# A hybrid encoder layer on one core: deferred use of transferred blocks, lanes tied behind the main stream, and earlier loads of token sums

## The chip, the cores and the metric

The kernel runs on one core of one Trainium2 chip. The core has a matrix engine (TensorE, PE), whose weight load runs beside its matmuls (PEld), a vector engine (VectorE, DVE), an activation engine (ScalarE, ACT), GpSimd (POOL) and SyncE (SP), and 16 DMA engines that move data between DRAM and the core's own memory. Each engine carries out its instructions in order; an instruction may wait for others on semaphores, and what is behind it waits too. SP issues nearly all transfers here, in one queue; POOL issues those that add into their target. The metric is the device time of one execution in microseconds (us).

## The reference

One encoder layer is computed for two sequences, a sample of 1024 tokens and a prompt of 512, with `d_model` 2048 and everything in float32:

```
h = rms_norm(x, norm_g);  z = h @ w_in                       # 2048 -> 5632
c_val, c_glu, c_gate, q, k, v, a_gate = split(z)             # 1024 x3, 1024, 256, 256, 1024
conv = silu(layer_norm(depthwise_conv31(c_val * sigmoid(c_glu)) + b)) @ w_pw * silu(c_gate)
attn = banded_sink_attention(rope(q), rope(k), v, sink) * silu(a_gate)   # 8 heads, 2 kv heads, window 128
y = rms_norm(x + concat(conv, attn) @ w_out, final_norm_g)
```

## The kernel before, in words

**Products.** Every float32 operand is split into a high and a low part, and a product is three passes on PE: high × high, high × low, low × high. The split of a weight block of 512 KB is a `Prep`: SP loads `raw`, ACT copies the high part (L343), DVE subtracts to get the low part (L344), and the result is an `hl` tile. There are three `raw` and three `hl` tiles.

**Units.** The input projection of the sample is cut into 22 column-block pairs: 8 of the convolution (`conv`) and 14 others (`rest`: gates, k and v, q with the attention gate). Each is worked on in two `Unit`s, one per half of the 2048 inputs. A `Unit` is a 2×2 scheme with seven products instead of eight: column blocks (two) by token halves (two, of 512 tokens). Weight sums (`sub`, DVE L132) and token sums (`T`, tiles t) are its operands. One product is four blocks of 128 by three passes, twelve matmuls (L178), into one of three banks in the order a b a c a c a; bank a is added into throughout, so the third product in a (step 4) may start only when the second (step 2) has been read, and so on. Reading a bank is the `tap`: after steps 0, 2, 3 and 6 an ACT copy (L203) into a new tile, after steps 1, 4 and 5 a DVE add (L205) to such a tile. The tiles are taken in turn from two pools, g and u, of four buffers each (`E`).

The tap of a product is traced in the midst of the next one. After steps 1, 4, 5 and 6 one of the unit's four output blocks is ready. In the first of the two `Unit`s of a pair it is stored to DRAM (`part_...`). In the second, POOL issues a transfer that adds the stored part into the tile (`add_into`, L334), and `done`, traced at once behind it, works on the sum: for conv `gated` (DVE L686, ACT L687, DVE L688 and the product L692), for q, k and v `rope` (DVE L753 to L756) or a scale, for gates and the attention gate a scale (DVE L701) and a silu (ACT L706). Then SP stores the block.

**Order of the stages.** 8 conv units on the first half of the inputs (to 188 us of the profile); 8 conv units on the second half, with `done` (188 to 378); 14 rest units on the second half (378 to 653); 14 rest units on the first half, with `done` (653 to 1049); then the prompt as `Job`s (L444, with its own taps, gates, q, k, v), and the `Post`s, which do the attention output and the last projection. The first two units of three of these stages run as a pair, product by product in turn. The 28 tiles of token sums hold one half of the inputs; at the end of the first and of the third stage `switch` replaces them, step by step: behind the unit's product of a step, `follow` makes that step's sum of the new half from four loaded tiles (`token_sum`, ACT L346 or L343, DVE L347 or L344) and then loads the four tiles of the next step (`load_sum`, L616) into the four p buffers. At the last unit before the prompt, another `follow` splits the prompt's x the same way from tiles `f` loaded one pair ahead (L1304).

**Lanes.** Depthwise convolution (`taps`: 29 DVE instructions L725 per block of 128 channels, 1024 wide), attention, and preparations such as the normalisation are generators on three `Lane`s. `tick`, called for each piece of a product, gives a lane credit, and the lane is traced a step further when it has enough. The scheduler orders each engine's instructions by priority, and by trace order within that: weight preparation, taps, `done` and token sums are `urgently` traced, with a higher priority than the lanes. A lane's instruction whose operands are ready early can be placed ahead of the stream's.

Of the kernel before, what the change touches and what calls it, by code (L numbers as in the profile page):

```python
# [2 lines left out]

# [32 lines left out]
SOON = 800  # L36
PM = 30
RUSH = 1.2
SPREAD = 3
RATES = (0.4, 0.9, 0.3, 1.0)  # L40
S1, S2, S3, S4, S5, S6, S7 = 5000, 6000, 9000, 7000, 3500, 2500, 6000
# [13 lines left out]
class Lane:  # L55


    def __init__(self, rate=1.0):
        self.todo = deque()
        self.rate = rate  # L60
        self.credit = 0.0
# [3 lines left out]

    def step(self):
        try:
            self.credit -= next(self.todo[0]) or 0
        except StopIteration:
            self.todo.popleft()  # L70

# [10 lines left out]
class Unit:  # L82
# [82 lines left out]
    def product(self, step, late):  # L165
        e, nc = self.e, self.e.nc
        p, o = OPERAND[step]
        i = self.at[p]
        e.w_prep(i + 1)
        hl = e.hl[i]  # L170
        n = BANK[step]
        if step in FRESH:
            self.bank[n] = e.PS(self.tags[n], [W])
        acc = self.bank[n]
        toks = e.T[SUMS[step]]
        for j in range(HALF):
            for q, (l, r) in enumerate(((0, 0), (0, 1), (1, 0))):
                nc.tensor.matmul(  # L178
                    acc,
                    hl[:, l, o, j, :],  # L180
                    toks[j][:, r],
                    start=step in FRESH and j == 0 and q == 0,
                    stop=step in LAST and j == HALF - 1 and q == 2,
                    skip_group_check=True,
                )
            if j == 0:
                for fn in late:
                    fn()
                e.w_prep(i + NHL)
            e.tick(3 * MM)  # L190
        if step in (1, 3, 5, 6):
            e.hl.pop(i)
        for fn in self.after.get(step, ()):
            fn()
        return [lambda: e.urgently(self.tap, step)]

    def tap(self, step):
# [8 lines left out]
        if step in (1, 4, 5, 6):  # L206
            part, d = self.part[n[0]][n[1]], self.d.pop(n)
            if self.done:

                e.add_into(d, part)  # L210
                self.done(n[0], n[1], d)
            else:
                e.store(part, d)

# [51 lines left out]
class Encoder:  # L266
    def __init__(self, ctx, tc, a):
# [8 lines left out]
        self.conv = Lane()  # L276
        self.attn = Lane()
        self.prep = Lane()
        self.lanes = [self.attn, self.conv, self.prep]
        self.turn = False  # L280
        self.banks = 0
# [67 lines left out]
    def tick(self, ns):  # L349
        for lane in self.lanes:  # L350
            lane.tick(ns)


    def constants(self):
# [63 lines left out]
    def run(self, items):  # L418
# [3 lines left out]
        for n, item in enumerate(items):  # L422
# [3 lines left out]
            if isinstance(item[0], Unit):  # L426
                for u in item:
                    u.open()
                for step in range(7):
                    for u in item:  # L430
                        late = u.product(step, late)
                continue
            job = item[0]
            job.acc = [self.acc()]
            nk = len(job.ks)
            for q in range(0, nk, 2 * HALF):
# [3 lines left out]
                for kk in range(2 * HALF):  # L440
# [9 lines left out]
                        )  # L450
                    if kk == 0:
                        self.w_prep(at + NHL)
                    if i in job.ticks:
                        job.ticks[i]()
                    self.tick(3 * MM)
# [58 lines left out]
class Sequence:  # L514
# [88 lines left out]
                e.store(self.sums_d[g, name][j], t)  # L603
            yield 6000

    def load_sum(self, name, g):
        e = self.e
        out = []
        for j in range(HALF):
            x = e.PT("p", NP, [W])  # L610
            if name in ("S1", "S2", "S3", "S4"):
                src = self.sums_d[g, name][j]
            else:
# [598 lines left out]
def encoder(ctx, tc, a):  # L1212
# [44 lines left out]
    def switch(unit, g):  # L1257
# [13 lines left out]
        for step in range(7):  # L1271
            unit.after[step] = [lambda step=step: follow(step)]

# [140 lines left out]
```

## Time and profile before

| | |
|---|---|
| three runs | 2347.69, 2348.84, 2353.24 us; median 2348.84 |
| the profiled execution | 2354.78 us; its span 2353.0 us |
| mean granted clock of PE | 0.965 |
| PE, DVE, ACT, POOL busy | 2186.8, 1613.1, 971.7, 76.9 us |
| DMA | 434.73 MB, mean 185 GB/s |
| the stretches 188 to 378, 378 to 653, 653 to 728.5, 728.5 to 1049, 1049 to the end | 190.4, 274.9, 75.2, 320.2, 1304.3 us |

The profile shows one execution. Busy time is time in which an engine works on an instruction; a share of it is of the whole span or of a window. Rows that read "X <- Y" give time that X stood idle until Y released it. Tiles are named by their pool, with their number left out. An instruction on a 1024-wide tile and one on a 512-wide tile of the same line stand in one group unless the shape is shown.

### The profile page before, as it was taken

To read this page: it belongs to the slowest core of one execution; us is meant where nothing else is said; L and a number is where in the kernel's file an instruction comes from. 1 tells how busy PE (TensorE), PEld (TensorE's weight loads), DVE (VectorE), ACT (ScalarE), POOL (GpSimd) and SP (SyncE) were. 2 spreads that over 40 slices of the span, in tenths; PEclk is the share of its full clock that TensorE was granted. 3 is DMA by queue.
4 is the path that set the end of the run, shared out by engine and by line. 5 is a ranking of instruction groups with operands and counts; after the bars stand their busy time and mean duration, and the time that the engine had idled before them with its cause. 6 is when DMAs were issued, how large, how long until landed. Compare 5 with 4: busy or idle time off the path is not lost.

```text
span 2353.0 us, 26578 instructions
## 1 busy us (share of the span) xinstructions
PE 2186.8 (93%) x9510; PEld 1781.2 (76%) x9510; DVE 1613.1 (69%) x2475; ACT 971.7 (41%) x1488; POOL 76.9 (3%) x92
## 2 busy tenths in 40 slices
PE   7999888999967878879999999999999999999998
PEld 5877667888845756667888888888787778888886
DVE  8657777999997777766636677867675367636343
ACT  5465324333443222244335454754464354423232
POOL 0001110000001111110000000000000000000000
PEclk8999899999989988889999999999999999999999
DMA  8988757664566556577655565455724438526442
GB/s 290 329 277 227 195 129 230 210 234 166 165 197 170 143 156 156 152 224 246 205 175 157 190 216 172 155 169 188 257 82 157 134 123 289 166 95 226 132 134 72
DMA packets 220421, 434.73 MB, mean 185 GB/s; under 512 B 20352, under 2 KB 78080, under 8 KB 220288
## 3 DMA queue, kind: packets, MB, share of 16 engines
q1 hardware_dynamic: 207616, 409.96, 52.5%
q0 software_dynamic: 12672, 23.07, 6.3%
q8 instruction: 74, 1.21, 0.2%
q14 instruction: 59, 0.48, 0.1%
HBM read 311.32 MB, written 121.63 MB: 184 GB/s over the span
## 4 chain that ended last, share of the span: by engine, by line
PE 57%; issue 22%; DMA 9%; DVE 7%; POOL 3%; ACT 2%; SPq 1%; POOLq 0%; ACTq 0%; DVEq 0%
PE a L444 17%; PE c L444 9%; PE b L444 9%; PE a L178 5%; DMA u<-q_d 3%; PE c L178 2%; PE s L835 2%; DVE f L725 2%; PE a L1174 2%; PE s L1174 2%; DVE hl L344 2%; POOL g L334 2%; PE pv L867 2%; DMA raw<-w_in 1%; DMA u<-ag_d 1%
## 5 line engine op out<-in xcount | busy, mean ns | idle before, releaser
L178 PE MATMUL a<-t,hl 128*128 128x512 f32 x1968 | 514.9, 415 | 105.0 <-DVE u L205 40.5
L178 PEld LDWEIGHTS a<-t,hl 128*128 128x128 f32 x1968 | 394.7, 203 | 204.3 <-DVE u L205 44.5
L444 PE MATMUL a<-t,hl 128*128 128x512 f32 x2112 | 506.4, 392 | 0.0
L444 PEld LDWEIGHTS a<-t,hl 128*128 128x128 f32 x2112 | 394.0, 188 | 79.9
L725 DVE SCALAR_TENSOR_TENSOR f<-f,c_w_dw,f 128x1024 f32<-128x1024 f32 (+1 forms) x464 | 452.4, 1013 | 2.7 <-ACT f L720 2.2
L343 ACT ACTIVATE hl<-raw 128x1024 fp32r<-128x1024 f32 (+1 forms) x279 | 275.9, 990 | 431.1 <-PE a L444 82.8
L344 DVE TENSOR_TENSOR hl<-raw,hl 128x1024 fp32r<-128x1024 f32 (+1 forms) x279 | 317.7, 1139 | 159.7 <-ACT hl L343 154.6
L178 PE MATMUL c<-t,hl 128*128 128x512 f32 x984 | 248.7, 400 | 20.1 <-DVE t L344 7.7
L444 PE MATMUL b<-t,hl 128*128 128x512 f32 x1056 | 258.5, 395 | 3.7 <-ACT t L346 1.9
L444 PE MATMUL c<-t,hl 128*128 128x512 f32 x1056 | 252.9, 391 | 0.0
L178 PEld LDWEIGHTS c<-t,hl 128*128 128x128 f32 x984 | 188.9, 193 | 65.2 <-DVE t L344 11.3
L444 PEld LDWEIGHTS b<-t,hl 128*128 128x128 f32 x1056 | 198.0, 190 | 45.2 <-ACT t L346 2.7
L444 PEld LDWEIGHTS c<-t,hl 128*128 128x128 f32 x1056 | 197.1, 188 | 39.9
L253 ACT ACTIVATE hl<-raw 128x1024 fp32r<-128x1024 f32 x88 | 93.0, 1058 | 118.3 <-PE a L444 45.3
L178 PE MATMUL b<-t,hl 128*128 128x512 f32 x492 | 119.2, 390 | 0.2
L178 PEld LDWEIGHTS b<-t,hl 128*128 128x128 f32 x492 | 92.2, 188 | 20.4 <-DVE t L347 0.8
L132 DVE TENSOR_TENSOR raw<-raw,raw 128x512 f32<-128x512 f32 x123 | 84.4, 686 | 23.9 <-DMA raw<-w_in 20.8
L344 DVE TENSOR_TENSOR a<-pt,a 128x512 fp32r<-128x512 f32 x64 | 44.1, 689 | 73.5 <-ACT a L343 73.3
L343 ACT ACTIVATE a<-pt 128x512 fp32r<-128x512 f32 x64 | 38.1, 595 | 90.3 <-PE pt L872 89.9
L1174 PE MATMUL a<-hl,t 128*128 128x512 f32 x192 | 74.7, 390 | 0.0
L203 ACT ACTIVATE u<-a 128x512 f32<-128x512 f32 x56 | 33.4, 596 | 97.7 <-PE a L178 95.9
L835 PE MATMUL s<-t,a 128*128 128x384 f32 (+1 forms) x288 | 59.4, 335 | 14.4 <-ACT a L343 13.8
(237 smaller groups left out, 2198.5 us busy)
## 6 DMA issues: line engine op xcount, KB each, us to landing
raw<-w_in SPq DMA_DIRECT2D x169, 512.0 KB, 5.0
raw<-w_out SPq DMA_DIRECT2D x64, 512.0 KB, 3.7
raw<-w_out SPq DMA_DIRECT2D x64, 256.0 KB, 3.3
raw<-w_pw SPq DMA_DIRECT2D x24, 512.0 KB, 3.5
f<-xT_s SPq DMA_DIRECT2D x38, 256.0 KB, 5.8
low_conv<-hl SPq DMA_DIRECT2D x16, 512.0 KB, 3.2
f<-x_s SPq DMA_DIRECT2D x16, 512.0 KB, 6.3
p<-sum_S SPq DMA_DIRECT2D x32, 256.0 KB, 3.8
```

Source lines behind the costliest of these rows:

```text
L132: self.e.nc.vector.tensor_tensor(out, x, y, ALU.subtract)
L178: nc.tensor.matmul(acc, hl[:, l, o, j, :], toks[j][:, r], start=step in FRESH and j == 0 and q == 0, stop=step in LAST and j == HALF - 1 a ...
L203: nc.scalar.activation(self.d[n], bank, AF.Copy)
L253: e.nc.scalar.activation(t[:, 0], raw, AF.Copy)
L334: self.nc.gpsimd.dma_start(dst, src, accum_op=ALU.add)
L343: nc.scalar.activation(hi, x, AF.Copy)
L344: nc.vector.tensor_tensor(lo, x, hi.bitcast(F32), ALU.subtract)
L444: nc.tensor.matmul(job.acc[0], hl[:, l, kk // HALF, kk % HALF, :], r, start=i == 0 and p == 0, stop=i == nk - 1 and p == 2,)
L725: nc.vector.scalar_tensor_tensor(t, h[:, j : j + T], w(j), t, ALU.mult, ALU.add)
L835: nc.tensor.matmul(ps[:, 0:n], qs[:, x, h], k[y][:, keys], start=p == 0, stop=p == 2)
L867: nc.tensor.matmul(pv, v[x][:, vs], pt[:, y], start=i == 0 and p == 0, stop=i == last and p == 2)
L1174: nc.tensor.matmul(acc, self.mix[self.KS[i]][:, m, b * P : (b + 1) * P], part[l].rearrange("p a b -> p (a b)"), start=i == 0 and p == 0, s ...
```

## The change

It has four parts. Line numbers in the changed kernel are 3 or 4 higher up to the tap (L178 becomes L181, L203 and L205 become L207 and L209), 6 higher for the weight preparation (L343, L344 become L349, L350), and 43 higher from the rope and the taps on (L725 becomes L768).

1. `done` is not traced behind `add_into`. It is put into `e.later` with a count, `LANDING = 4`; `turn_over`, called once in each product right behind the tap and the weight preparation, lowers the counts and traces what has come to zero. What is left is traced at the first `Job`.
2. `mark` notes the last DVE and the last ACT instruction traced so far (at each `turn_over`); `behind` ties everything traced within it to come after these two in the engines' order. Lane steps and deferred `done`s are traced in it.
3. In `switch`, loads run two steps ahead instead of one, and for odd steps go into tiles of pool `a`, two pairs of two, instead of the four of `p`.
4. The prompt's x goes to tiles of pool `a`, and is loaded three pairs ahead instead of one.

```diff
+LANDING = 4
 class Lane:
-    def __init__(self, rate=1.0):
+    def __init__(self, e, rate=1.0):
+        self.e = e
...
     def step(self):
         try:
-            self.credit -= next(self.todo[0]) or 0
+            with self.e.behind():
+                self.credit -= next(self.todo[0]) or 0
...
                 for fn in late:
                     fn()
                 e.w_prep(i + NHL)
+                e.turn_over()
             e.tick(3 * MM)
...
                 e.add_into(d, part)
-                self.done(n[0], n[1], d)
+                e.later.append([LANDING, lambda: self.done(n[0], n[1], d)])
...
+    def mark(self):
+        found = {}
+        for i in reversed(self.nc.cur_bb.bb.instructions):
+            if i.engine in (mybir.EngineType.DVE, mybir.EngineType.Activation):
+                found.setdefault(i.engine, i)
+                if len(found) == 2:
+                    break
+        self.marks = list(found.values())
+    @contextmanager
+    def behind(self):
+        with ExitStack() as stack:
+            for i in self.marks:
+                stack.enter_context(self.tc.issue_after(i))
+            yield
+    def turn_over(self, all=False):
+        self.mark()
+        for n, entry in enumerate(self.later):
+            entry[0] -= 1
+        while self.later and (all or self.later[0][0] <= 0):
+            with self.behind():
+                self.urgently(self.later.popleft()[1])
...
+            while self.later:
+                self.turn_over(True)
             job = item[0]
...
                     if kk == 0:
                         self.w_prep(at + NHL)
+                        self.turn_over()
...
-    def load_sum(self, name, g):
+    def load_sum(self, name, g, wide):
+        if wide:
+            pairs = [e.A([2, W], F32) for _ in range(HALF // 2)]
+            tiles = [t[:, j] for t in pairs for j in range(2)]
+        else:
+            tiles = [e.PT("p", NP, [W]) for _ in range(HALF)]
...
-            held[step] = sample.load_sum(SUMS[step], g)
+            held[step] = sample.load_sum(SUMS[step], g, step % 2)
...
-            if step < 6:
-                load(step + 1)
-        unit.before.append(lambda: load(0))
+            if step < 5:
+                load(step + 2)
+        def begin():
+            load(0)
+            load(1)
+        unit.before.append(begin)
...
     def load_two(j):
-        t = e.F([2, TP])
+        t = e.A([2, TP], F32)
...
-            if k + 2 < ND and k % 2 == 0:
-                load_two(k + 2)
+            if k + 6 < ND and k % 2 == 0:
+                load_two(k + 6)
...
-        load_two(0)
+        for j in (0, 2, 4):
+            load_two(j)
```

How instructions move, at three places.

DVE, in a unit of q and the attention gate (stretch 728.5 to 1049), from the tap of the block u_5926 to its `done` (the scale, L701). Before:

```order
L205 TENSOR_TENSOR u_5926<-a_5836,u_5926 128x512
L132 TENSOR_TENSOR raw_5896<-raw_5896 128x512
L132 TENSOR_TENSOR raw_5854<-raw_5854,raw_5967 128x512
L205 TENSOR_TENSOR g_5911<-c_5907,g_5911 128x512
L725 SCALAR_TENSOR_TENSOR f_4887<-f_4844,c_w_dw,f_4887 128x1024
L701 TENSOR_TENSOR u_5926<-u_5926,f_1681 128x512
```

The same block, g_5906, in the changed kernel:

```order
L209 TENSOR_TENSOR g_5906<-a_5816,g_5906 128x512
L796 TENSOR_TENSOR u_5926<-u_5843,f_5085 64x512
L797 TENSOR_TENSOR u_5926<-u_5843,f_5085 64x512
L135 TENSOR_TENSOR raw_5828<-raw_5828,raw_5947 128x512
L798 TENSOR_TENSOR u_5843<-u_5843,f_5084 128x512
L209 TENSOR_TENSOR g_5885<-c_5881,g_5885 128x512
L799 TENSOR_TENSOR u_5843<-u_5843,u_5926 128x512
L350 TENSOR_TENSOR hl_5950<-raw_5947,hl_5950 128x1024
L768 SCALAR_TENSOR_TENSOR f_4953<-f_4911,c_w_dw,f_4953 128x1024
L350 TENSOR_TENSOR hl_5970<-raw_5867,hl_5970 128x1024
L768 SCALAR_TENSOR_TENSOR f_4954<-f_4911,c_w_dw,f_4954 128x1024
L744 TENSOR_TENSOR g_5906<-g_5906,f_1683 128x512
```

Four rows lay between the tap and its `done`; now ten do, among them the `done` of the block before (L796 to L799) and two weight preparations (L350). The tile of that earlier block, u_5843, is in use until then.

SP's queue at the second switch, near 653 us (p and a: the loaded tiles; sum_S: stored token sums; xT_s: the sample's x; raw, and a_4909 in the changed kernel: weights). Before:

```order
L112 DMA raw_5264<-w_in 128x1024
L741 DMA f_5098<-cos 128x1024
L616 DMA p_4863<-xT_s 128x512
L337 DMA conv_d_4_76<-f_4423 128x1024
L616 DMA p_4865<-xT_s 128x512
L616 DMA p_4867<-xT_s 128x512
L616 DMA p_4869<-xT_s 128x512
L616 DMA p_4902<-sum_S_0_117 128x512
```

In the changed kernel:

```order
L343 DMA part_gate_10_262<-u_5094 128x512
L659 DMA p_4857<-sum_S_0_117 128x512
L659 DMA p_4858<-sum_S_1_118 128x512
L659 DMA p_4859<-sum_S_2_119 128x512
L659 DMA p_4860<-sum_S_3_120 128x512
L343 DMA conv_d_4_76<-f_4438 128x1024
L115 DMA a_4909<-w_in 128x1024
L659 DMA a_4976<-sum_S_0_125 128x512
```

The loads of the second step's tiles (from x) have left this place for one some 200 rows earlier in SP's queue, where those of the first step stood already, in the stretch 188 to 378; those of the third step (sum_S_0_117 and on) have moved up; the load of cos no longer stands ahead of the sums; the weights of the pair's second unit (a_4909) stand behind four sums and the store of a convolution block.

DVE in the prompt, at a block of attention (tiny, p: softmax; hl: weight preparation). Before:

```order
L853 TENSOR_TENSOR tiny_8404<-tiny_8404,tiny_8403 128x4
L854 RECIPROCAL tiny_8405<-tiny_8404 128x4
L857 TENSOR_SCALAR p_8438<-p_8438,tiny_8405 128x384
L857 TENSOR_SCALAR p_8444<-p_8444,tiny_8405 128x384
L255 TENSOR_TENSOR hl_8385<-raw_8383,hl_8385 128x512
L344 TENSOR_TENSOR a_8567<-pt_8562,a_8567 128x512
```

In the changed kernel:

```order
L259 TENSOR_TENSOR hl_8373<-raw_8371,hl_8373 128x512
L896 TENSOR_TENSOR tiny_8392<-tiny_8392,tiny_8391 128x4
L897 RECIPROCAL tiny_8393<-tiny_8392 128x4
L900 TENSOR_SCALAR p_8426<-p_8426,tiny_8393 128x384
L900 TENSOR_SCALAR p_8432<-p_8432,tiny_8393 128x384
L350 TENSOR_TENSOR a_8555<-pt_8550,a_8555 128x512
```

The weight preparation, which stood behind four rows of softmax, now stands ahead of them.

More of the change, by code (lines that the diff above doesn't have):

```diff
@@ L1 @@
 from collections import deque
-from contextlib import ExitStack
+from contextlib import ExitStack, contextmanager
 import concourse.bass as bass
@@ L275, in __init__ @@
         self.count = 0
-        self.conv = Lane()
-        self.attn = Lane()
-        self.prep = Lane()
+        self.conv = Lane(self)
+        self.attn = Lane(self)
+        self.prep = Lane(self)
+        self.marks = []
+        self.later = deque()
         self.lanes = [self.attn, self.conv, self.prep]
@@ L604, in sums_ahead @@
             yield 6000
-    def load_sum(self, name, g):
+    def load_sum(self, name, g, wide):
         e = self.e
         out = []
+        if wide:
[3 more added lines that the diff above has]
+            tiles = [e.PT("p", NP, [W]) for _ in range(HALF)]
         for j in range(HALF):
-            x = e.PT("p", NP, [W])
+            x = tiles[j]
             if name in ("S1", "S2", "S3", "S4"):
```

## The prediction

> **What bounds the kernel now.** I read the page's head first, then busy time by stage, then the waits of the one stage that loses most, then its rows in order of time. All line numbers are those of the kernel before.
>
> Head of the page: TensorE (PE) is busy nearly throughout, so the gain lies where it is not.
>
> ```profile
> PE 2186.8 (93%) x9510; PEld 1781.2 (76%) x9510; DVE 1613.1 (69%) x2475; ACT 971.7 (41%) x1488; POOL 76.9 (3%) x92
> ```
>
> Busy time in five stretches; the columns are the window, its length, the busy us of PE, its weight load, VectorE (DVE), ScalarE (ACT) and GpSimd (POOL), PE's granted clock, the DMA share and GB/s. The stretches are: conv units with `done`; units without `done`; the two units at the switch of token sums, with `done`; twelve single units with `done`; the rest.
>
> ```profile
> 188.00:378.40 190.40, 166.55 (x674) 133.53 (x673) 142.91 (x186) 73.45 (x107) 27.12 (x31) 0.93 0.68 181
> 378.40:653.30 274.90, 270.31 (x1181) 221.76 (x1180) 259.01 (x306) 102.64 (x139) 0.87 (x1) 0.99 0.61 203
> 653.30:728.50 75.20, 47.35 (x174) 34.80 (x173) 62.94 (x77) 29.89 (x45) 5.29 (x6) 0.85 0.63 194
> 728.50:1048.70 320.20, 260.33 (x1023) 208.16 (x1022) 235.03 (x298) 96.59 (x139) 42.59 (x49) 0.88 0.62 165
> 1048.70:2353.00 1304.30, 1276.59 (x5791) 1051.04 (x5789) 785.62 (x1414) 570.06 (x909) 0.88 (x1) 0.99 0.52 170
> ```
>
> Where a unit has no `done` (second row), PE is 98% busy at clock 0.99, with DVE 94% busy. Where it has one, PE falls to 87, 63 and 81%, and the clock to 0.93, 0.85 and 0.88. The last row has 1276.6 of 1304.3 us busy: at most 28 us to win in more than half of the run. The waits of the twelve units, PE's and then DVE's (engine, line and what it waited for; total us, times, longest):
>
> ```profile
> PE a L178 <- DVE u L205: 40.5, 9, 7.6
> PE a L178 <- DVE g L205: 10.7, 2, 5.8
> ```
> ```profile
> DVE u L753 <- DMA g<-part_q: 41.2, 16, 3.7
> DVE u L701 <- DMA u<-part_q: 12.3, 8, 1.8
> DVE g L701 <- DMA g<-part_gate: 9.6, 4, 4.9
> DVE u L753 <- DMA g<-part_kv: 5.3, 3, 2.1
> DVE u L701 <- DMA u<-part_gate: 5.3, 3, 2.7
> DVE u L701 <- DMA u<-part_kv: 4.2, 2, 2.4
> DVE g L701 <- DMA g<-part_q: 3.0, 3, 1.6
> ```
>
> PE waits for L205, the add by which DVE empties a bank; DVE itself stands 80.9 us (the sum of the seven rows) at the first instruction of `done`, for the transfer that adds the stored part. One unit in order of time (start, length, engine, instruction, idle before it):
>
> ```profile
> 800.74 5.73 PE L178 MATMUL a<-t,hl 128*128 128x512 f32 x24 [1.12 <-DVE u L205]
> 807.42 0.86 POOL L334 DMA_DIRECT2D g<-part_q  x1 [3.67 <-ACT g L203]
> 813.55 0.69 DVE L753 TENSOR_TENSOR u<-g,f 64x512 f32<-64x512 f32 x1 [3.50 <-DMA g<-part_q]
> 814.58 2.88 PE L178 MATMUL a<-t,hl 128*128 128x512 f32 x12
> 817.30 2.88 PE L178 MATMUL c<-t,hl 128*128 128x512 f32 x12
> 817.86 0.89 POOL L334 DMA_DIRECT2D g<-part_q  x1 [9.58 <-DVE g L205]
> 822.68 0.69 DVE L753 TENSOR_TENSOR u<-g,f 64x512 f32<-64x512 f32 x1 [2.22 <-DMA g<-part_q]
> 827.05 0.68 DVE L205 TENSOR_TENSOR u<-a,u 128x512 f32<-128x512 f32 x1
> 827.79 8.12 PE L178 MATMUL a<-t,hl 128*128 128x512 f32 x24 [7.61 <-DVE u L205]
> ```
>
> A product starts every 2.72 us (817.30 − 814.58), so a unit of seven needs 19.04 us and twelve 228.5; the stretch takes 320.2. The transfer issued at 807.42 is first used at 813.55, 6.1 us later, the one of 817.86 at 822.68, 4.8 us later; at both DVE has idled, and the adds behind it come late. After 7.61 us of idleness 24 matmuls take 8.12 instead of 5.73 us: the lower clock costs 2.4 more. So DVE waits for transfers, PE for DVE, and then runs slower.
>
> **The change, part by part.** *Deferred `done`, twelve units.* `done` is traced four products after the tap, three after the tap's own trace: 3 × 2.72 = 8.2 us against landings of 4.8 to 6.1. By the order of instructions, 7 to 12 DVE rows now lie between a tap and its `done`. Their prices, as spacing from start to start, are:
>
> ```profile
> 657.89 10.85 DVE L725 SCALAR_TENSOR_TENSOR f<-f,c_w_dw,f 128x1024 f32<-128x1024 f32 x9
> ```
>
> 1.2 us for a 1024-wide row (10.85 / 9), half of it, 0.6, for a 512-wide one (which lasts 0.68 by the row at 827.05): some 7 to 9 us in a row, so the transfer has landed. I take all 80.9 away: 320.2 − 80.9 = 239.3, which is DVE's own work (235.0 busy) and so the floor by DVE; PE's is 228.5. What is late next? `done`, four rows of 0.7 for a rotated block, now stands among the weight preparation, which has a loop of its own: the low part L344 is stored, SP then issues the load of the next raw weights, DVE subtracts, prepares, and so on.
>
> ```profile
> raw<-w_in SPq DMA_DIRECT2D x23, 512.0 KB, 5.6
> ag_d<-g SPq DMA_DIRECT2D x8, 256.0 KB, 5.2
> ```
>
> By the rows between the first L132 and the second preparation of a unit I count 11.1 to 16.0 us of DVE; with 0.3 to issue and 5.6 to land, 17 to 22 us against 239.3 / 12 = 19.9 per unit. Three of eleven units go over, by 2.1 each: +6.3. A g or u buffer is also held longer now: the next tap that takes it waits for a store such as the second row's. It is not in the trace as a wait; its bounds are nothing, where the store has landed, and 5.2 us in each unit. I take 0.5 per unit, near the lower end, because there are four buffers of each: +6. Together 239.3 + 6.3 + 6 = 251.6, **−68.6**; the ends are −81 (DVE's floor) and −12 (320.2 − 239.3 − 6.3 − 12 × 5.2 = 12.2 left).
>
> *Deferred `done`, conv units (188 to 378).* DVE's waits there for the added parts:
>
> ```profile
> DVE u L692 <- DMA u<-part_conv: 13.6, 6, 3.7
> DVE g L686 <- DMA g<-part_conv: 12.7, 7, 2.2
> DVE u L686 <- DMA u<-part_conv: 7.5, 5, 2.2
> DVE g L692 <- DMA g<-part_conv: 2.6, 1, 2.6
> ```
>
> 36.4 us. DVE's 142.9 busy leaves it under PE's 8 × 19.04 = 152.3, so PE's floor decides. 190.4 − 36.4 = 154.0; with +6 for the same two queues, 160: **−30** (0 to −38).
>
> *Token sums ahead, the switch.* DVE, PE and SP there:
>
> ```profile
> 668.67 0.73 DVE L347 SCALAR_TENSOR_TENSOR t<-p,c_norm_g,t 128x512 fp32r<-128x512 f32 x1
> 669.47 1.65 PE L178 MATMUL a<-t,hl 128*128 128x512 f32 x3 [15.63 <-DVE t L347]
> 668.76 0.33 SPq L741 DMA_DIRECT2D f<-cos  x1
> ```
>
> PE idles 15.63 us for the first new sum, which stands on DVE behind eleven conv taps (L725) that the new order leaves ahead of it. I give that wait no gain. SP's queue was held until 668.76 by a load whose buffer those taps held, and the sums behind it came late; now three steps of sums are issued ahead of it. Setting the loads, the sums and the products of these two units on one clock by the rows above, the pair ends at about 718 instead of 728.5: **−10** (0 to −24; 75.2 − 24 = 51 is still over DVE's share without the taps). What is pushed back instead is the raw load of the pair's second unit, behind four sums and a conv store on SP; its preparation is not first needed until the pair's next product.
>
> *Tie, and x ahead.* With lanes put behind the stream's instructions, a lane row no longer runs ahead of a tap. Two stalls of that kind, the first unit of the second stretch and the last before the prompt:
>
> ```profile
> 393.07 4.38 PE L178 MATMUL a<-t,hl 128*128 128x512 f32 x12 [3.50 <-ACT u L203]
> 1044.10 4.81 PE L178 MATMUL a<-t,hl 128*128 128x512 f32 x12 [4.96 <-DVE g L205]
> ```
>
> 3.50 and 4.96, with 4.38 − 2.72 = 1.7 and 2.1 of lower clock: 12.2 in all; I take half, **−6** (0 to −12). Prompt and posts (1304.3 us) I cost at nothing: PE's rows keep their places to within a matmul, and the tie moves DVE rows by one or two; what hides that is ACT at 44% and DVE at 60%. Without that cover: the slower rival below.
>
> Sum: −68.6 − 30 − 10 − 6 = −114.6. The profiled execution took 2354.8, its span 2353.0; 2354.8 − 114.6 = 2240.2. The median is 5.9 under that execution, so the forecast is 2240.2 − 5.9 ≈ **2235**. All terms at their good ends, −81 − 38 − 24 − 12 = −155, give 2194.
>
> **Rivals.** *The transfers land later than three products.* With the stream faster, the same bytes move in 79% of the time (251.6 / 320.2), so DMA share 0.62 would be 0.79.
>
> ```profile
> g<-part_q POOLq DMA_DIRECT2D x24, 256.0 KB, 4.6
> raw<-w_in SPq DMA_DIRECT2D x12, 512.0 KB, 5.3
> ```
>
> For: the landing of 4.6 leaves 3.6 us of slack under 8.2, and the two waits traced above began at 6.1 and 4.8. Against: the second row is from 20 to 160 us, at a DMA share of 87.6%, and the same raw load lands in 5.3, no later than here. If half of the DMA waits come back (40 of 80.9 and 18 of 36.4), the time is 2235 + 58 = 2293; a third gives 2274. The Trainium skill ("DMA: Bandwidth & Descriptors", section "Issuing engines are not separate DMA queues") says that transfers of all issuing engines run on the same 16 DMA engines and interleave. By that rule, as an estimate, landings stretch with the share, 5.6 × 0.79 / 0.62 = 7.1 for raw weights and 5.9 for the added part: the latter is still under 8.2, and the former makes the raw loop 1.5 longer, eight of eleven units over by 15.8 in all instead of 6.3, which would give 2245. The stage at 87.6% does not agree with it.
>
> *A new wait takes its place.* The buffers of g and u, held three products longer, or the store queue, stop the taps: 2.5 us, half of the store's 5.2, in each of 20 units is +50: 2285. For: a tap now needs a buffer whose store is issued only after the later `done`. Against: four of each, and 5.2 is less than two products.
>
> *To the floors.* No loop, no buffer wait, the switch's idleness gone too: about 2200.
>
> *It does nothing*, because the scheduler puts `done` back: 2345. Against: the order shows the rows moved.
>
> *Slower: lanes tied too far back in the prompt.* A lane's DVE and ACT rows come behind the weight preparation of the stream, which waits for a buffer that PE frees; attention's matmuls on PE then wait for them, and PE's queue is in order.
>
> ```profile
> PE s L835 <- ACT a L343: 13.8, 12, 3.2
> ACT hl L343 <- PE a L444: 82.8, 34, 4.7
> ```
>
> For: ACT waits 82.8 us in preparations for PE, 2.4 each and up to 4.7, and attention rows now stand behind these. 24 attention blocks each paying two products' time, 2 × 2.72 = 5.44, make 131, over the 114.6 gained: 2235 + 131 = 2366. It decides from 114.6 / 24 = 4.8 us per block. Against: PE waits only 13.8 us for that line now, in 12 places, and its rows keep their places.
>
> **How the numbers follow.** Forecast 0.60; late landings 0.12; a new wait 0.10; floors 0.06; between 2300 and 2340 by parts of these 0.04; nothing 0.03; slower 0.05. The forecast's own range is 2205 to 2262, by the bounds of the terms nearer to it. To leave out no more than 2 in 10 the range takes in the two rivals of 0.12 and 0.10, which leaves 0.18 to the other four: **2205 to 2295**. About 0.3%, 7 us, is what a measurement of this kernel can tell from no change: faster 0.91, within it 0.04, slower 0.05.
>
> **What would show it.** Right: in the twelve units DVE's waits for `part_q` near nothing, the units' length about 21 us, PE clock above 0.95; conv units at about 160; the pair at the switch some 10 shorter with the 15.6 us idleness before it unchanged; the prompt within 5 us. The loop shows as DVE L132 waiting for the raw load, a buffer wait as L203 or L205 waiting for a store. Wrong: waits on `part_q` of more than 20 us in all (late landings); new PE waits on L835's line; or PE idleness in the conv units that no transfer explains.

## The result, and the profile after

The changed kernel takes 2256.84 us (median of four, 2254.54 to 2256.94) against 2348.27 before (median of four, 2345.27 to 2353.24): ratio 0.9606, 95% interval 0.9588 to 0.9624, or 91.4 us less. The forecast was 2235 with a range of 2205 to 2295: the sign and the main mechanism are as forecast, and the gain is 91 instead of 114. Its profiled execution took 2256.94 us, its span is 2255.2. One single execution among all those reported below, the profiled one of e7 (LANDING = 6), ran at a mean granted clock of 0.75, took 2703.75 us and is left out of that kernel's ratio.

The head of the page after the change, and busy time in the five stretches, cut at the same places of the program (columns as in the prediction):

```profile
PE 2153.3 (95%) x9510; PEld 1759.3 (78%) x9510; DVE 1610.3 (71%) x2475; ACT 972.0 (43%) x1488; POOL 77.1 (3%) x92
```
```profile
186.60:346.50 159.90, 152.13 (x662) 123.22 (x661) 132.87 (x173) 64.25 (x91) 27.00 (x31) 1.00 0.75 206
346.50:621.20 274.70, 270.11 (x1181) 220.50 (x1179) 266.07 (x313) 106.84 (x148) 1.01 (x2) 1.00 0.61 208
621.20:686.70 65.50, 44.21 (x168) 34.98 (x167) 62.19 (x78) 28.65 (x43) 5.95 (x7) 0.84 0.67 208
686.70:942.20 255.50, 240.24 (x1027) 194.50 (x1026) 223.00 (x291) 98.51 (x142) 41.13 (x48) 0.97 0.75 207
942.20:2255.20 1313.00, 1279.95 (x5793) 1052.67 (x5791) 797.29 (x1425) 570.84 (x909) 1.76 (x2) 0.99 0.52 169
```

| stretch | before | forecast | after | difference |
|---|---|---|---|---|
| conv units, first half (to 188.0, now 186.6) | 188.0 | – | 186.6 | −1.4 |
| conv units with `done` | 190.4 | 160 | 159.9 | −30.5 |
| rest units without `done` | 274.9 | part of −6 | 274.7 | −0.2 |
| the pair at the second switch | 75.2 | 65 | 65.5 | −9.7 |
| twelve single units with `done` | 320.2 | 251.6 | 255.5 | −64.7 |
| prompt and posts | 1304.3 | 1304 | 1313.0 | +8.7 |

The differences add up to −97.8, as do the two spans (2353.0 and 2255.2). That is 6.4 more than the medians differ by, since the profiled execution before was 6.5 us above its median and the one after only 0.1. In the conv units and the twelve PE's clock has risen from 0.93 and 0.88 to 1.00 and 0.97, and the DMA share from 0.68 and 0.62 to 0.75.

Waits in the twelve units (686.7 to 942.2) after the change, PE's and then DVE's; columns: engine, tile, line and releaser, us in all, times, longest:

```profile
PE a L181 <- DVE g L209: 11.3, 7, 3.7
PE c L181 <- ACT g L207: 2.5, 2, 1.9
```
```profile
DVE raw L135 <- DMA raw<-w_in: 8.7, 6, 2.4
DVE raw L135 <- issue: 6.1, 3, 3.5
...
DVE u L744 <- DMA u<-part_gate: 3.4, 1, 3.4
...
DVE u L796 <- DMA g<-part_q: 1.5, 3, 0.8
```

Of 80.9 us of waits for added parts 4.9 are left. DVE's first wait is now for raw weights. One block of q in order of time: its last add, the transfer, and its `done` 9.2 us after the transfer's issue (852.15 − 843.00), without a wait; the row of PE is the same step (from one unit to the next) that idled 7.61 us and took 8.12 before, though of a unit four later.

```profile
841.92 0.68 DVE L209 TENSOR_TENSOR u<-b,u 128x512 f32<-128x512 f32 x1
843.00 0.87 POOL L340 DMA_DIRECT2D u<-part_q  x1 [5.88 <-DVE u L209]
846.76 0.60 ACT L207 ACTIVATE g<-c 128x512 f32<-128x512 f32 x1 [1.81 <-DMA ag_d<-g]
852.15 0.69 DVE L796 TENSOR_TENSOR u<-u,f 64x512 f32<-64x512 f32 x1
852.17 5.78 PE L181 MATMUL a<-t,hl 128*128 128x512 f32 x24 [1.15 <-DVE g L209]
```

The row of ACT in between shows the cost on the other side: a tap that waits 1.81 us for a g buffer, until a stored block has landed.

The second switch. DVE runs eleven taps ahead of the first new token sum, PE waits for that, and then for the preparation of the second unit's weights, whose load SP issues at 638.56:

```profile
620.19 13.23 DVE L768 SCALAR_TENSOR_TENSOR f<-f,c_w_dw,f 128x1024 f32<-128x1024 f32 x11
634.14 5.06 PE L181 MATMUL a<-t,hl 128*128 128x512 f32 x11  [12.70 <-DVE t L353]
638.56 0.33 SPq L115 DMA_DIRECT2D a<-w_in  x1
645.88 1.81 PE L181 MATMUL s<-t,hl 128*128 128x512 f32 x4  [3.98 <-ACT hl L349]
663.27 1.22 PE L181 MATMUL s<-t,hl 128*128 128x512 f32 x2  [4.62 <-ACT hl L349]
```

And the prompt's only large wait of PE:

```profile
PE s L878 <- ACT a L349: 18.9, 12, 5.1
```

### The profile page after: what moved, and what is told of

The parts are those of the page before. It is cut to its first block, busy times and chain, and to the rows that moved or that the text cites. A ratio compares the mean times of both kernels' runs of the same rounds, so it can differ in the third digit from the quotient of the medians.

```text
span 2255.2 us, 26606 instructions
## 1 busy us (share of the span) xinstructions
PE 2153.3 (95%) x9510; PEld 1759.3 (78%) x9510; DVE 1610.3 (71%) x2475; ACT 972.0 (43%) x1488; POOL 77.1 (3%) x92
## 4 chain that ended last, share of the span: by engine, by line
PE 53%; DMA 6%; DVE 4%; ACT 2%; issue 1%; SPq 0%; ACTq 0%; DVEq 0%
PE a L481 17%; PE b L481 9%; PE c L481 9%; PE a L181 3%; DMA u<-q_d 3%; PE s L878 2%; PE a L1217 2%; PE s L1217 2%; PE pv L910 2%; DMA u<-ag_d 1%; PE pt L915 1%; PE c L181 1%; PE pv L1217 1%; PE b L1217 1%; PE c L1217 1%
## 5 line engine op out<-in xcount | busy, mean ns | idle before, releaser
L181 PE MATMUL a<-t,hl 128*128 128x512 f32 x1968 | 483.1, 397 | 42.5 <-DVE g L209 19.3
L481 PE MATMUL a<-t,hl 128*128 128x512 f32 x2112 | 507.6, 392 | 0.0
L181 PEld LDWEIGHTS a<-t,hl 128*128 128x128 f32 x1968 | 374.7, 192 | 132.0 <-DVE g L209 28.1
L481 PEld LDWEIGHTS a<-t,hl 128*128 128x128 f32 x2112 | 393.8, 188 | 79.6
L768 DVE SCALAR_TENSOR_TENSOR f<-f,c_w_dw,f 128x1024 f32<-128x1024 f32 (+1 forms) x464 | 451.2, 1010 | 2.9 <-ACT f L763 2.8
L349 ACT ACTIVATE hl<-raw 128x1024 fp32r<-128x1024 f32 (+1 forms) x279 | 276.3, 990 | 399.9 <-PE a L481 74.2
L350 DVE TENSOR_TENSOR hl<-raw,hl 128x1024 fp32r<-128x1024 f32 (+1 forms) x279 | 317.5, 1138 | 170.2 <-ACT hl L349 169.2
L181 PE MATMUL c<-t,hl 128*128 128x512 f32 x984 | 243.7, 395 | 10.1 <-ACT t L349 4.7
L181 PEld LDWEIGHTS c<-t,hl 128*128 128x128 f32 x984 | 186.5, 190 | 52.8 <-ACT t L349 5.9
L181 PE MATMUL b<-t,hl 128*128 128x512 f32 x492 | 119.0, 390 | 0.0
L181 PEld LDWEIGHTS b<-t,hl 128*128 128x128 f32 x492 | 92.6, 188 | 19.3
L350 DVE TENSOR_TENSOR a<-pt,a 128x512 fp32r<-128x512 f32 x64 | 44.0, 687 | 69.3 <-ACT a L349 69.1
L878 PE MATMUL s<-t,a 128*128 128x384 f32 (+1 forms) x288 | 60.3, 339 | 19.5 <-ACT a L349 18.9
L207 ACT ACTIVATE u<-a 128x512 f32<-128x512 f32 x66 | 39.4, 596 | 90.9 <-PE a L181 84.0
L349 ACT ACTIVATE a<-pt 128x512 fp32r<-128x512 f32 x64 | 38.1, 595 | 88.7 <-PE pt L915 88.3
```

Of the source, the lines that this page charges most:

```text
L181: nc.tensor.matmul(acc, hl[:, l, o, j, :], toks[j][:, r], start=step in FRESH and j == 0 and q == 0, stop=step in LAST and j == HALF - 1 a ...
L207: nc.scalar.activation(self.d[n], bank, AF.Copy)
L349: nc.scalar.activation(hi, x, AF.Copy)
L350: nc.vector.tensor_tensor(lo, x, hi.bitcast(F32), ALU.subtract)
L481: nc.tensor.matmul(job.acc[0], hl[:, l, kk // HALF, kk % HALF, :], r, start=i == 0 and p == 0, stop=i == nk - 1 and p == 2,)
L768: nc.vector.scalar_tensor_tensor(t, h[:, j : j + T], w(j), t, ALU.mult, ALU.add)
```

## The experiments

Each kernel was timed in three rounds beside the kernel before on the same chip, but for the last one; that kernel took 2354 to 2357 us there, so ratios are compared, with their intervals. "In us" is the ratio times 2348.27. Stretches are of one execution each, so a difference of a few us between two of them can be chance. For the stretches I use one more cut that can be counted in every trace: ACT makes four tap copies in each unit, 176 in all, so the 33rd, 65th and 129th copy mark the ends of the first, second and (third with the pair) stretches; the end of the twelve units is the end of the last matmul of a unit. By this cut the lengths, in us of the profiled executions, are (e7 is missing: its profile is of the execution that is left out):

| | conv with `done` | rest and pair | twelve | prompt, posts | ratio |
|---|---|---|---|---|---|
| before | 190.4 | 351.0 | 316.0 | 1304.1 | 1 |
| the change | 163.4 | 339.6 | 252.6 | 1312.9 | 0.9606 |
| e1 no tie | 188.3 | 349.1 | 289.5 | 1303.1 | 0.9856 |
| e2 no deferral | 192.1 | 352.3 | 296.5 | 1311.9 | 0.9949 |
| e3 landing 3 | 166.1 | 354.2 | 248.5 | 1314.6 | 0.9657 |
| e4 loads as before | 168.3 | 345.9 | 259.8 | 1312.1 | 0.9665 |
| e5 attention untied | 164.6 | 339.6 | 249.5 | 1309.8 | 0.9590 |
| e6 conv rate 0.7 | 165.6 | 318.4 | 257.3 | 1311.8 | 0.9511 |
| e8 both of these | 165.1 | 317.5 | 256.2 | 1309.0 | 0.9501 |
| e9 only `done` tied | 164.5 | 347.9 | 256.7 | 1309.4 | 0.9625 |
| e10 landing 3, rate 0.7 | 168.1 | 324.3 | 255.1 | 1317.6 | 0.9521 |
| e11 rates 0.7 and 0.2 | 164.8 | 316.8 | 248.4 | 1315.1 | 0.9485 |
| e12 landing 6 | 162.7 | 365.1 | 243.1 | 1305.6 | – |

**Does the deferral do it, or the tie?** First the change without the tie:

```diff
     def behind(self):
         with ExitStack() as stack:
-            for i in self.marks:
-                stack.enter_context(self.tc.issue_after(i))
             yield
```

> The deferral and the early loads stay, the tie is gone: lanes and deferred `done`s are traced where the change traces them, but nothing holds them behind the stream's instructions. In the order of instructions the `done` of a q unit then stands only 3.0 to 4.8 us of DVE rows behind its tap (3.0 to 3.6 before the change, 7.2 to 10.2 with the change). My theory, that the gain is the distance between tap and `done` on DVE against a landing of 4 to 7 us: most of the DVE waits for the added parts stay, 50 to 80 us of them in the twelve units and 20 to 35 in the conv units, and the time is 2310 to 2345. Rival, that tracing `done` three products later is what gains and the tie adds little: at most 2270, and DVE's waits for part_q under 20 us.

Ratio 0.9856 (0.9828 to 0.9885), 2314 in us. DVE's waits in its twelve units, the four largest:

```profile
DVE g L742 <- DMA g<-part_q: 17.8, 16, 3.1
DVE u L794 <- DMA u<-part_q: 11.6, 8, 1.9
DVE u L794 <- DMA g<-part_q: 9.5, 7, 2.2
DVE g L742 <- DMA g<-part_gate: 5.8, 4, 2.0
```

With the smaller rows, 54.5 us of waits for added parts are still there (80.9 before), and 35.5 (36.4 before) in the conv units, whose stretch is as long as before (188.3). The rival falls: to write the `done` later in the program does not by itself place it later. In the order of this kernel it stands, as the expectation says, only 3.0 to 4.8 us of DVE rows behind its tap: `done` is traced as urgent work, and the scheduler takes it forward. What was deferred is its place in the text, not the instruction.

Then the tie without the deferral:

```diff
                 e.add_into(d, part)
-                e.later.append([LANDING, lambda: self.done(n[0], n[1], d)])
+                self.done(n[0], n[1], d)
```

> `done` is traced right behind the transfer as before the change; the tie of the lanes and the early loads stay. `done` stands 1.2 to 3.6 us behind its tap in the order. My theory: the waits for the added parts stay as before (about 80 us in the twelve units, 36 in the conv units); only the switch gains, about 10: 2325 to 2345. Rival, that lane rows ahead of the taps were what made PE wait and the tie alone gives most of the gain: at most 2290.

Ratio 0.9949 (0.9924 to 0.9974), 2336: in the expected range, but by luck in part. In the conv units DVE waits as before:

```profile
DVE g L729 <- DMA g<-part_conv: 18.1, 7, 4.9
DVE u L735 <- DMA u<-part_conv: 13.6, 6, 3.6
DVE u L729 <- DMA u<-part_conv: 5.8, 5, 2.8
```

In the twelve units 61.6 us of these waits are left where about 80 were expected, and the units are 19.5 us shorter. The switch, which was to gain 10, gains nothing (352.3 against 351.0 in the rest and the pair): PE waits 13.8 us for the first token sum and 15.0 for the preparation of the second unit's weights. The prompt is 7.8 longer.

One part alone gains 1.4%, the other 0.5%, both with the loads in them; together they gain 3.9%. They are one mechanism in two halves. Which half of the tie is needed, that of `done` or that of the lanes, is asked by:

```diff
     def step(self):
         try:
-            with self.e.behind():
+            with ExitStack():
                 self.credit -= next(self.todo[0]) or 0
```

> As the changed kernel, but no lane is tied; only the deferred `done`s are traced behind the mark. In the order `done` then stands 7.2 to 11.4 us of DVE rows behind its tap in most units, as with the full change (3.0 to 4.8 without any tie). Theory: the tie of `done` is the half that counts, since without it the scheduler moves `done` forward to its tap; lanes may run ahead of a tap now and then: 2250 to 2270, and the prompt's stretch back near 1303 to 1306. Rival, that the lanes' tie is what shortens PE's waits for the taps: 2290 or more.

Ratio 0.9625 (0.9603 to 0.9646), 2260, which can't be told from the full change. The conv units (164.5) and the twelve (256.7) are within 5 us of it. DVE's waits for added parts in the twelve are 13.7 us, where e1 has 54.5. So the tie of `done` carries the gain, and the lanes' tie is worth little there; the rest and the pair are 8.3 longer than with it (347.9 against 339.6). The prompt did not come back to 1303: beside shorter waits for the scores there is a new one at its start:

```profile
PE s L878 <- ACT a L349: 12.8, 10, 2.5
PE b L481 <- ACT t L352: 8.3, 1, 8.3
```

**How far must `done` be?** `LANDING = 4` was replaced by 3, and by 6.

> LANDING = 3 in place of 4: `done` two products (5.4 us) behind its transfer, and 5.4 to 7.2 us of DVE rows behind its tap in a q unit. My theory: that is about the landing, so small waits of up to 1.5 us come back at some of the 48 `done`s in the twelve units, but the buffers of g and u are held one product shorter: 2255 to 2275, waits for the added parts 10 to 30 us in the twelve units. If the landing has become longer under the higher DMA share (0.75 now against 0.62), waits of 40 us and more, 2280 to 2300.

Ratio 0.9657 (0.9635 to 0.9679), 2268; the time is in the expected range, but the loss is not where it was expected. Waits for added parts in the twelve units are 13.2 us, most of them here (first row, DVE), and yet these units are no longer than with 4. The rest and the pair are 14.6 longer; eighteen taps, five and thirteen with one other row between them, run on DVE ahead of the first token sum, from 627.93 to 650.05 us, and PE waits for it (second row):

```profile
DVE u L744 <- DMA u<-part_q: 11.4, 7, 2.9
```
```profile
PE a L181 <- DVE t L353: 21.7, 1, 21.7
```

> LANDING = 6: `done` five products (13.6 us) behind its transfer, 11 to 16 us of DVE rows behind its tap in a q unit. All waits for the added parts should be gone. Theory that the buffers of g and u and the stores behind `done` are the next limit: taps on DVE and ACT wait for buffers whose blocks are not stored, 1 to 3 us in each of 20 units, 2275 to 2310. Rival, that a distance above the landing costs nothing: 2252 to 2262.

Ratio 0.9650 (0.9624 to 0.9677), 2266, between the ranges of the theory and of the rival, and slower than with 4 by about the width of the intervals. For a profile that can be compared the kernel was run once more:

> LANDING = 6 once more, for a profile: it was about 10 us slower than LANDING = 4. Theory that tiles of g and u are held too long: in the twelve units ACT's copies L207 or DVE's adds and rope wait for stores (q_d, ag_d) or for the `done` of earlier blocks, 10 us or more that the changed kernel does not have. Rival, that the loss is at the second switch, where more taps stand ahead of the first token sum: PE's wait there 16 us or more and the twelve units within 3 us of 255.

One time, 2265.74. The theory of the buffers falls: with `done` five products behind, the twelve units are the shortest of all kernels here, 243.1. ACT does wait for stores there,

```profile
ACT u L207 <- DMA q_d<-u: 20.6, 11, 4.8
```

but not 10 us more than the changed kernel does (18.9, the row of ag_d in the next section). The loss is in the rest and the pair, 365.1 against 339.6, where PE waits for the first token sum, for a small matmul of the prompt's norm that a lane puts into PE's queue, and for adds:

```profile
PE a L181 <- DVE t L353: 18.3, 1, 18.3
...
PE a L181 <- DVE g L209: 8.2, 8, 2.2
PE s L548 <- DVE u L547: 7.4, 1, 7.4
```

In the change the three are 12.7, 3.1 and nothing, which accounts for 18.1 of the 25.5 us. The rival had named the place, but not that the twelve units would gain.

**What are the loads worth?** Token sums one step ahead in p, x one pair ahead in f, the rest of the change kept:

```diff
-            held[step] = sample.load_sum(SUMS[step], g, step % 2)
+            held[step] = sample.load_sum(SUMS[step], g, 0)
...
-            if step < 5:
-                load(step + 2)
+            if step < 6:
+                load(step + 1)
...
             load(0)
-            load(1)
...
-        t = e.A([2, TP], F32)
+        t = e.F([2, TP])
...
-            if k + 6 < ND and k % 2 == 0:
-                load_two(k + 6)
+            if k + 2 < ND and k % 2 == 0:
+                load_two(k + 2)
...
-        for j in (0, 2, 4):
-            load_two(j)
+        load_two(0)
```

> Token sums are loaded one step ahead into p again, and the prompt's x one pair ahead into f; deferral and tie stay. My theory, the loads are worth the 10 us that the pair at the second switch gained (75.2 to 65.5): 2262 to 2272, nearly all of it between 621 and 687 us, the prompt's start within 3. Rival, that the pair gained by the deferral and the tie and the loads do nothing: within 3 of 2257.

Ratio 0.9665 (0.9642 to 0.9688), 2270, in the expected range, and above the change by 0.6% with intervals that don't overlap. The place was only partly right: of the profiled difference 6.3 lie in the rest and the pair, 7.2 in the twelve units, 4.9 in the conv units and 3.2 before them; the profiled execution, 2278.23 us, is also the slowest of the four of this kernel (the others 2271.55 to 2274.34). In the rest and the pair PE waits for the switch as long as in the change: 21.3 us for token sums and nothing for the second unit's preparation, against 12.7 and 8.6. The early loads moved the wait from one to the other. Why the stretch, and the units behind it, are longer without them was not traced.

**Where do the 8.7 us in the prompt come from?**

```diff
-            with self.e.behind():
+            with self.e.behind() if self is not self.e.attn else ExitStack():
                 self.credit -= next(self.todo[0]) or 0
```

> As the changed kernel, but steps of the attention lane are not tied; the conv and preparation lanes and the deferred `done`s are. Theory: the tie of attention is what made the stretch from the prompt's first matmul to the end longer (1313 against 1304 us; every run with the tie has 1312 to 1315 there, the one without it 1303): 1303 to 1306 in that stretch, and 2247 to 2252 in all, waits of the scores' matmuls on PE back from 18.9 to about 14. Rival, that the prompt is longer because what the sample's part no longer did in its own time falls on it: the stretch stays above 1310 and the time at 2257.

Ratio 0.9590 (0.9565 to 0.9616), 2252: not to be told from the change. The stretch is 1309.8, a third of the way back, and PE's waits for the scores are 15.5 instead of 18.9 us. Kernels with every tie have 1305.6 to 1317.6 in that stretch, a spread larger than the effect in question. That the tie of attention costs some 3 us fits. Two other causes are made unlikely by other rows of the table. The eleven taps that fall into the prompt since the change (40 there instead of 29) are not it: e6, next, moves 28 more there, and its stretch is 1311.8. Nor is it the deferral or the early x: e2, with the ties and without the deferral, has 1311.9, e4 without the early x 1312.1, and e1, with both and without any tie, 1303.1. So the longer prompt goes with the ties; but e12 has every tie and 1305.6, and how the rest of the 8.7 comes about is open.

**The stall that was left at the second switch.** Eleven taps ahead of the first token sum are a backlog of the conv lane in the stretch before, where DVE is busy 266.1 of 274.7 us.

```diff
-RATES = (0.4, 0.9, 0.3, 1.0)
+RATES = (0.4, 0.7, 0.3, 1.0)
```

> As the changed kernel, but the conv lane's rate in the third stretch is 0.7 instead of 0.9. In the order no run of taps stands ahead of the first new token sum on DVE any more (11 in the changed kernel); 29 more taps move behind that sum. Theory: PE's wait of 12.7 us for the first token sum, and the low clock after it, go, and the taps find room on DVE in the prompt (61% busy): 2240 to 2248. Rival, that the taps come due in the prompt and delay its work there as much: 2257 or more.

Ratio 0.9511 (0.9491 to 0.9531), 2233, clearly faster than the change, and by more than was expected. PE goes from the last product of the stretch into the pair without a wait (24 matmuls in a, the last of the one and the first of the other):

```profile
620.15 5.62 PE L181 MATMUL a<-t,hl 128*128 128x512 f32 x24
```
```profile
615.13 0.33 SPq L115 DMA_DIRECT2D a<-w_in  x1
```

The rest and the pair lose 21.2 us, more than the wait of 12.7: the waits for the second unit's preparation are down from 8.6 to 2.6 too, with SP issuing its load ahead of the pair (the row of SPq above) instead of at 638.56; most of the other 2.5 is PE's busy time (310.7 for 313.7, at a granted clock of 0.99 for 0.97). The taps cost nothing in the prompt (1311.8 against 1312.9), where DVE's busy time rose from 797 to 832 us.

> Both of the two: attention not tied, conv rate 0.7 in the third stretch. If both theories hold and their places are apart (the prompt, the second switch) the gains add: 2232 to 2242. If the freed taps fall on the attention's part of the prompt, the sum is smaller: 2245 to 2252.

Ratio 0.9501 (0.9477 to 0.9524), 2231, at the good end of what was expected; the step from rate 0.7 alone is within the intervals, so that the untied attention adds anything is not shown.

> LANDING = 3 together with the conv rate of 0.7 in the third stretch. With LANDING = 3 alone the twelve single units were no longer than with 4 (248.5 against 252.5 us by the taps' times), and what was lost lay at the second switch, where 15 taps stood ahead of the first token sum and PE waited 21.7 us for it. If that is the whole loss, the two settings together are as fast as rate 0.7 with LANDING = 4: 2233 to 2245. If two products are too few for the landing, it stays 10 or more above: 2250 to 2260.

Ratio 0.9521 (0.9499 to 0.9543), 2236: with the backlog gone LANDING = 3 and 4 can't be told apart. So what LANDING = 3 lost lay at the switch, and two products, 5.4 us, are nearly enough for these landings. (The expectation's 15 taps were 18.)

> Conv rate 0.7 in the third stretch and 0.2 instead of 0.3 in the fourth, LANDING = 4, all ties. In the twelve units DVE is busy 223 of 255.5 us, and PE still waits 25 to 27 us in all for DVE's add L209. Theory: DVE's load sets these units; with a third of their taps moved to the prompt (12 to 25 fewer taps, 1.2 us each) the units come nearer to PE's 228.5: 2228 to 2238. Rival, the loop of raw loads sets them: no change within 4 of 2241.

Ratio 0.9485 (0.9467 to 0.9503), 2227, 1.3% under the change and the fastest kernel here. The twelve units are 248.4 against 257.3 in the profiled executions, with fourteen taps fewer (24 for 38) and shorter waits of PE for DVE's add, 16.3 us at rate 0.3 (e6, first row; the expectation has 25 to 27) and 10.3 at 0.2:

```profile
PE a L181 <- DVE g L209: 16.3, 8, 3.0
```
```profile
PE a L181 <- DVE g L209: 10.3, 7, 2.6
```

That is what the theory of DVE's load says, but it is not shown: the kernels with rate 0.3 and LANDING = 4 have 249.5 to 259.8 there, in the total the step from rate 0.7 alone is within the intervals (0.9467 to 0.9503 and 0.9491 to 0.9531), and DVE still waits 19.5 us for raw weights, 22.8 in e6, so the rival's loop is not ruled out.

## Why the prediction was right, point by point

- *What bounds the kernel.* Right. DVE stood at `done` for the added part, PE for DVE, and e1 and e2, where most of DVE's wait stays, gain 1.4 and 0.5%, while e9, where it goes, gains 3.8. With the 117.3 us of these waits (80.9 + 36.4) down to 4.9 in the twelve units and 1.8 in the conv units, the stretches lose 95.2.
- *Deferred `done`, twelve units: −68.6 forecast, −64.7 measured.* The sum held, but its terms less well. Its start was DVE's own 239.3 as a floor; DVE is busy 223.0 us there now, since eleven taps (38 for 49, 1.2 us each) have moved out of the stretch into the prompt (40 for 29). So part of the gain was not foreseen, and the rest was mis-sized the other way: the forecast stood 16.6 above DVE's busy time (251.6 − 235.0), the measurement 32.5 (255.5 − 223.0). Of the raw loop (+6.3 in the sum) and the buffers (+6): DVE waits 14.8 us for raw weights and their issue, and PE waits 13.8 for taps (11.3 and 2.5), which is the most that it can feel of both. The stretch is 27.0 above PE's 228.5. That the forecast is met within 4 us owes something to luck.
- *Buffers held longer.* The wait is there, as the prediction said it would show:

```profile
ACT g L207 <- DMA ag_d<-g: 18.9, 7, 3.8
```

 18.9 us on ACT, 1.6 per unit where I had taken 0.5, but PE itself waits only 2.5 us for these copies. The rival that made it decisive (2285) fell, and e12, which holds tiles still longer, has the shortest units.
- *Conv units: 160 forecast, 159.9 measured.* Right, at PE's clock of 1.00.
- *The switch: −10 forecast, −9.7 measured.* Right in size, and the wait for the first sum stayed, as forecast, at 12.7 instead of 15.6. The cause is right only in part, so the size is partly luck. In the rest and the pair the change gains 11.4 by the table of experiments, of which the loads account for 6.3 (e4); e1 and e2 have the loads and gain 1.9 and −1.3. One step was wrong: that the raw load of the second unit, pushed back, would still be in time. PE waits 3.98 + 4.62 = 8.6 us for its preparation.
- *Tie and early x: −6 forecast.* Failed. Of its two stalls, the one at 393.07 is gone, but its stretch changed by −0.2 only. The one at 1044.10 lies before 1048.7, in the twelve units, so the −68.6 had already taken it: it was counted twice. Costing the prompt at nothing was the largest miss: 8.7, more than the 5 that were to show the prediction right, of which 5.1 are longer waits for the scores (18.9 for 13.8). That looks like the slower rival's mechanism, at 0.2 us per block (5.1 / 24) instead of the 5.44 that it needed; e5 and e9 shorten these waits by 3.4 and 6.1.
- *Late landings.* Fell. The rows of these transfers between 690 and 940 us, then that of the u tiles before the change (740 to 1040):

```profile
raw<-w_in SPq DMA_DIRECT2D x25, 512.0 KB, 6.0
g<-part_q POOLq DMA_DIRECT2D x24, 256.0 KB, 4.7
...
u<-part_q POOLq DMA_DIRECT2D x8, 256.0 KB, 5.7
```
```profile
u<-part_q POOLq DMA_DIRECT2D x8, 256.0 KB, 4.2
```

 At a DMA share of 0.75 these medians are 0.4, 0.1 and 1.5 us longer, all under 8.2. But the two rows of `part_q` are not of the same blocks before and after: the first transfer of each q unit goes into a g tile before the change and into a u tile after it, the second the other way round. All 32 together, worked out from their single landings in the two traces, take 4.8 us on average before and 5.5 after, the longest 6.6 and 8.0, so the slack under 8.2 was nearly used up. That transfers of all issuing engines run on the same 16 DMA engines, which the Trainium skill states ("DMA: Bandwidth & Descriptors", section "Issuing engines are not separate DMA queues"), agrees in direction. The stretching by the share, my estimate from it, said 7.1 for raw weights and 5.9 for the added parts, too much for the first (6.0) and near for the second.
- *"It does nothing, because the scheduler puts `done` back."* Given 0.03 for the change as a whole, and rightly, but e1 shows that this is just what happens without the tie: I had costed deferral and tie as separate terms, and the −98.6 that I gave to the deferral belongs to the two together.

The misses add up: +3.9 in the twelve units, +6.0 for the gain that did not come, +8.7 in the prompt, +0.3 in the pair, −0.5, −0.2 and −1.4 in the other three stretches make the 16.8 us between −114.6 and −97.8. The other 5 us between 2235 and the median of 2256.84 are the 5.9 that the forecast took off because the profiled execution before stood above its median; the one after does not (2240.2 − 5.9 is 2234.3, not quite 2235).

## What to carry to other kernels

Where an engine that works in order stands at the first use of a transfer, put enough of its other work between, counted in us of its own rows against the transfer's landing, and look in the final order whether it stays there: a scheduler that places urgent work early can undo a deferral that is only written later in the program, as in e1. Such a change moves load in time, so the next stall may come from backlog: look for runs of low-priority work ahead of the first instruction of a new stage, and give that work its time where the engine is idle.

## What the runs showed of the hardware that was not expected

How long an adding transfer takes here depends on its place in the unit more than on the DMA share. The four of a q unit, in order of issue, landed in 4.5, 4.2, 4.2 and 6.1 us before the change (medians of eight units, share 0.62) and in 5.7, 4.1, 4.8 and 7.4 after it (share 0.75): the second did not change, the other three did. The rows by tile name hide this, since the blocks had changed tiles.

A short idleness of PE can be enough for the lower clock. After 2.31 us of it 24 matmuls took 7.38 us, at a granted clock of 0.68 from 791.9 to 795.0; after 2.46 us, at 262.37, they took 5.74.

```profile
791.92 7.38 PE L181 MATMUL a<-t,hl 128*128 128x512 f32 x24 [2.31 <-DVE g L209]
262.37 5.74 PE L181 MATMUL a<-t,hl 128*128 128x512 f32 x24 [2.46 <-DVE g L209]
```
